# Two-layer attention trunk on one core: later use of turned rows, and the gate's key sums added from DRAM instead of by a matmul

## The chip, the core and the metric

The kernel runs on one core of one Trainium2 chip. The metric is the device time of one execution in microseconds (us), lower is better. The core has five engines with queues of their own, each in order: TensorE (PE; PEld is its weight load), VectorE (DVE), ScalarE (ACT), GpSimd (POOL) and SyncE (SP, which only issues transfers). ScalarE and GpSimd issue transfers too.

## The reference

256 tokens of width 2048 pass two layers. Layer 0 mixes by forgetting attention (FoX, 16 heads of 128), layer 1 by dilated attention (8 heads, three dilation groups, values of width 256). Each mixer is followed by a squared-ReLU MLP of width 8192. All is float32. What matters here, cut from the reference:

```python
# FoX: c is the running sum over tokens of log sigmoid of a gate, one per head
log_f = jax.nn.log_sigmoid((f + b_f).astype(jnp.float32))
c = jnp.cumsum(log_f, axis=1)
c_keys = jnp.transpose(c, (0, 2, 1))
...
s = jnp.einsum('bqhd,bkhd->bhqk', q_i, k) * scale      # q, k RMS-normed per head
s = s + jnp.transpose(c_i, (0, 2, 1))[..., None] - c_keys[:, :, None, :]
s = jnp.where(causal, s, -jnp.inf)
p = jax.nn.softmax(s, axis=-1)
o = jnp.einsum('bhqk,bkhd->bqhd', p, v)
```

So each score gets the query's sum c_i, less the key's sum c_keys, and the causal mask.

## The kernel before

**Products.** Tokens lie in two tiles of 128 (`NT`). Weights come in as raw blocks of 256 rows by 512 columns (`load`, L288, SyncE's queue). `split` makes two parts of each: `wh` by a cast on ScalarE (L309) and the rest `wl` on VectorE (L310), five buffers of each. `product_steps` (L340 to L342) multiplies, for each of 16 values of k and both token tiles, high by high, high by low and low by high: six matmuls of 128x512 a step. After each second step a new block is split, and after each step the clock of the jobs ticks.

**Jobs.** All other work is written as generators. `yield 3` lets three steps pass, and `yield ("fk", j)` waits until that name is done. When a job runs decides where its instructions stand in the engines' queues. `behind(x)` puts a job's instructions behind the instruction x on x's engine; `issued["cast"]`, `issued["cut"]` and `issued["product"]` are the latest cast (L309), cut (L310) and product (L342).

**Queries and keys (`qk_chain`).** After the product of 512 columns, squares on ScalarE give each head's norm; three steps later VectorE normalises (L532) and transposes 32x32 blocks (L540), SyncE writes the blocks to DRAM (L544), and GpSimd's queue reads them back turned (L545, `qn`). After 10 steps, and then 2 and 2, the turned rows of the first and of the second token tile are scaled and copied (L554, L561) on ScalarE, and the rest is taken on VectorE (L563). Then ("fq", j), ("fk", j) or ("dqk", q4, g) is done. The work tiles of a chain are four of the five buffers of the tag "w".

**FoX heads.** Four groups j of four heads: product of queries, of keys, of values, 16 steps each. `gate_chain` makes the running sums `c_q` (by token) once, and from them `negc`, in which rows 0 to 15 and 32 to 47 hold the high and low parts of the 16 heads' negative sums over the keys. `make_sel(j)` builds on GpSimd a selector with ones in the two rows of each head. `fox_head` waits for queries, keys, gate and mask and a number of steps, then L746 multiplies selector and `negc` into a score bank (128x384), on which the scores are accumulated: 128 columns for the first token tile (L657), 256 for the second in three parts (L660). L754 adds `c_q` and the mask on VectorE. Softmax follows; the probabilities are turned by way of DRAM on ScalarE's queue (`p_turned`, L610 and L614), or for the last two heads by TensorE, split (`p_split`, L623 and L625), and multiplied with the values (`pv`, L593, L594). The score banks are two (`ps_sc`), shared with `pv`.

**Dilated heads.** `dil_head` does the same for three groups of scores (L806 adds a table of distances); four rounds q4 of two heads, with three chains of queries and keys in each round. The output projections use the heads in order, the last ones at k = 12 to 15.

Of the kernel before, what the change touches and what calls it, by code (L numbers as in the profile page):

```python
# [89 lines left out]
def trunk(ctx: ExitStack, tc, x, fox_w_in, fox_b_f, fox_q_gain, fox_k_gain, fox_w_out, dil_w_in,  # L90
# [422 lines left out]
    def qk_chain(acc, tag, key, parts):  # L513

        yield (tag, "rstd")
        sq = []
        for t in range(NT):
            s = work.tile([P, NC], F32, tag="w", name=f"sq_{key}_{t}", bufs=5)
            nc.scalar.activation(halves(s), by_column(acc[t]), AF.Square, scale=rstd[tag][:, t:t + 1])
            sq.append(s)  # L520
        ss = small.tile([P, NT, 4], F32, tag="ss", name=f"ss_{key}")
        for t in range(NT):
            nc.vector.tensor_reduce(ss[:, t, :], sq[t].rearrange("p (h d) -> p h d", h=4), AX.X, ALU.add)
        nc.vector.tensor_scalar(ss, ss, 1.0 / P, EPS, ALU.mult, ALU.add)
        rq = small.tile([P, NT, 4], F32, tag="rq", name=f"rq_{key}")
        nc.gpsimd.tensor_tensor(rq, ss, mhalf.rearrange("p (t h) -> p t h", t=NT), ALU.pow)
        yield 3
        qn = []
        for t in range(NT):
            nc.vector.tensor_scalar_mul(rq[:, t, :], rq[:, t, :], rstd[tag][:, t:t + 1])  # L530
            q = work.tile([P, 4, P], F32, tag="w", name=f"qn_{key}_{t}", bufs=5)
            nc.vector.tensor_mul(q.rearrange("p (h g) d -> p h g d", h=2),  # L532
                                 acc[t].rearrange("p (g d h) -> p h g d", h=2, g=2),
                                 rq[:, t, :].rearrange("p (h g) -> p h g", h=2).unsqueeze(3).to_broadcast([P, 2, 2, P]))
            qn.append(q)


        for t in range(NT):
            turned = sq[t].rearrange("p (j h r) -> p j h r", j=4, h=4)
            nc.vector.transpose(turned.rearrange("p j h r -> p h j r"),  # L540
                                qn[t].rearrange("p h (j c) -> p h j c", c=32))
            blocks = dram.tile([4, 32, 4, P], F32, tag="blocks", name=f"blocks_{key}_{t}", bufs=4)
            for i in range(4):
                nc.sync.dma_start(blocks[:, :, i, :].rearrange("j c x -> c j x"), sq[t][32 * i:32 * i + 32].rearrange("p (j x) -> p j x", j=4))  # L544
            nc.gpsimd.dma_start(qn[t], blocks.rearrange("j c i x -> (j c) (i x)").rearrange("p (h d) -> p h d", h=4))  # L545
        yield 10
        for t in range(NT):
            yield 2
            for n, (c, nh, gcol, (whole, hi, lo)) in enumerate(parts):
                keys = hi.shape[2] == S  # L550
                src = qn[t].rearrange("p i (h r) -> p h i r", h=4)[:, c // P:c // P + nh]
                to = sq[0].rearrange("p (n i x) -> p n i x", n=2, i=2)[:, n] if t else whole
                with behind(issued["cast"]):
                    nc.scalar.activation(to.rearrange("p h (i r) -> p h i r", i=4), src, AF.Copy, scale=gain[:, gcol:gcol + 1])  # L554
                if t == 0 and not keys:
                    continue
                at = slice(t * P, (t + 1) * P) if keys else slice(0, P)

                a, b = (x[:, :, at].rearrange("p i (h n) -> p i h n", h=2) for x in (hi, lo))
                of = to.rearrange("p i (n h) -> p i h n" if keys else "p i (h n) -> p i h n", h=2)  # L560
                nc.scalar.copy(a, of)  # L561
                with behind(issued["cut"]):
                    nc.vector.tensor_sub(b, of, a.bitcast(F32))  # L563
        jobs.done.add(key)
# [85 lines left out]
        v_hi, v_lo = (work.tile([P, NC], F32R, tag=f"v{x}", name=f"{name}{x}", bufs=1) for x in "hl")  # L650
        return whole, v_hi, v_lo

    def scores(ps, t, q, k, i, onto=False):

        (q_whole, q_hi, q_lo), (k_whole, k_hi, k_lo) = q, k
        if t == 0:
            nc.tensor.matmul(ps[:, 0:P], q_whole[:, i, :], k_whole[:, i, :], start=not onto, stop=not onto)  # L657
            return
        for x, (a, b) in enumerate(((q_hi, k_hi), (q_hi, k_lo), (q_lo, k_hi))):
            nc.tensor.matmul(ps[:, P:3 * P], a[:, i, :], in_turn(b[:, i, :], P // 2), start=not onto and x == 0, stop=x == 2)  # L660


    c_q = const.tile([P, NT, FH], F32, name="c_q")

    negc = const.tile([P, 3 * P], F32R, name="negc")

    def gate(tag):
        pf = ps_sc.tile([2 * FH, S], F32, tag="sc", name="pf")
# [5 lines left out]
    def gate_chain(tag, pf):  # L674
# [46 lines left out]
        pct = ps_sc.tile([FH, S], F32, tag="sc", name="pct")  # L721
        for t in range(NT):
            nc.tensor.transpose(pct[:, t * P:(t + 1) * P], c_q[:, t, :], ident)
        ct = work.tile([FH, S], F32, tag="s", name="g_ct", bufs=S_BUFS)
        nc.vector.tensor_scalar(ct, pct, -1.0, None, ALU.mult)
        zero = work.tile([P, 3 * P], F32, tag="s", name="g_zero", bufs=S_BUFS)
        nc.vector.memset(zero, 0.0)
        nc.vector.tensor_copy(negc, zero)
        keys = by_column(ct, P // 2)
        high, low = (negc[at:at + FH, :] for at in (0, 32))  # L730
        nc.vector.tensor_copy(halves(high[:, P:], P // 2), keys)
        nc.vector.tensor_sub(halves(low[:, P:], P // 2), keys, halves(high[:, P:], P // 2).bitcast(F32))
        for part in (high, low):
            nc.vector.tensor_copy(part[:, 0:P], part[:, P:2 * P].bitcast(F32))
        jobs.done.add("gate")

    def fox_head(j, hh, qT, kT, vt, sel):
        h = 4 * j + hh
        yield ("fq", j)
        yield ("fk", j)  # L740
        yield "gate"
        yield "mask"
        yield ((0, 2, 4, 7) if j == 3 else (0, 4, 8, 12))[hh] + 2
        ps = ps_sc.tile([P, 512], F32, tag="sc", name=f"sc_f{h}")
        with behind(issued["product"]):
            nc.tensor.matmul(ps[:, 0:3 * P], sel[:, hh, :], in_turn(negc, P // 2), start=True, stop=False)  # L746
        for t in range(NT):
            scores(ps, t, qT[hh // 2], kT[hh // 2], hh % 2, True)
        s = work.tile([P, 3 * P], F32, tag="s", name=f"s_f{h}", bufs=S_BUFS)
        nm = small.tile([P, NT], F32, tag="nm", name=f"nm_f{h}")  # L750
        den = small.tile([P, NT], F32, tag="den", name=f"den_f{h}")
        spans = [slice(0, P), slice(P, 3 * P)]
        for t in range(NT):
            nc.vector.scalar_tensor_tensor(s[:, spans[t]], ps[:, spans[t]], c_q[:, t, h:h + 1],  # L754
                                           tables["mask"][:, spans[t]], ALU.add, ALU.add)
        for t in range(NT):
            nc.vector.tensor_reduce(nm[:, t:t + 1], s[:, spans[t]], AX.X, ALU.max, negate=True)
        yield 1
# [11 lines left out]
        else:  # L770
            turned = yield from p_turned(s, f"f{h}")
            yield ("fv", j)
            pt_sb = p_split(turned, f"f{h}")
        yield 2
        if ("f", h // 2) not in oT:
            oT["f", h // 2] = tuple(
                act.tile([P, 2, S], F32R, tag=f"aT{x}", name=f"oTf{x}_{h}", bufs=KC // 2) for x in "hl")
# [1 line left out]
        yield from pv(pt_sb, vt, [hh * P], [hi[:, h % 2, :]], [lo[:, h % 2, :]], f"f{h}")  # L779
        jobs.done.add(("of", h))  # L780

    def make_sel(j):
        sf = work.tile([P, 4, P], F32, tag="w", name=f"self{j}", bufs=5)
        nc.gpsimd.memset(sf, 0.0)
        for base in (0, 32):
            nc.gpsimd.affine_select(out=sf, in_=sf, compare_op=ALU.not_equal, fill=1.0, base=-base - 4 * j,
                                    pattern=[[-1, 4], [0, P]], channel_multiplier=1)
        sel = work.tile([P, 4, P], F32R, tag="sel", name=f"sel{j}", bufs=1)
        nc.vector.tensor_copy(sel, sf)
        return sel  # L790


    def dil_head(q4, i, qTs, kTs, vt):
        h = 2 * q4 + i
        for g in range(3):
            yield ("dqk", q4, g)
        yield (3 if q4 == 3 else 6) * i + 2
        s = work.tile([P, 3, 3 * P], F32, tag="sd", name=f"sd{h}", bufs=1)
        for g in range(3):
            yield ("table", g)  # L800
# [26 lines left out]
        else:  # L827
            turned = yield from p_turned(p, f"d{h}")
            yield ("dv", q4)
            pt_sb = p_split(turned, f"d{h}")  # L830
        yield 2
        hi, lo = (act.tile([P, 2, S], F32R, tag=f"aT{x}", name=f"oTd{x}_{h}", bufs=KC // 2) for x in "hl")
        oT["d", h] = hi, lo
        yield from pv(pt_sb, vt, [i * S, i * S + P], [hi[:, 0, :], hi[:, 1, :]], [lo[:, 0, :], lo[:, 1, :]], f"d{h}")
# [148 lines left out]

    tag = "n0"
    for j in range(4):
        sel = make_sel(j)
        qT = [heads_pair(f"fqT{j}_{i}", i, False) for i in range(2)]
        kT = [heads_pair(f"fkT{j}_{i}", 3 + i, True) for i in range(2)]
        vt = values(f"fv{j}")
        product(keys_h(tag), lhs_h(tag), lambda acc: qk_chain(  # L990
            acc, tag, ("fq", j), [(0, 2, FOX_G, qT[0]), (2 * P, 2, FOX_G, qT[1])]))
        if j == 0:
            jobs.need("wf")
            gate(tag)
        product(keys_h(tag), lhs_h(tag), lambda acc: qk_chain(
            acc, tag, ("fk", j), [(0, 2, FOX_G + 1, kT[0]), (2 * P, 2, FOX_G + 1, kT[1])]))

        for hh in range(4):
            jobs.spawn(fox_head(j, hh, qT, kT, vt, sel))
        product(keys_h(tag), lhs_h(tag), lambda acc: v_chain(acc, tag, ("fv", j), vt))  # L1000

    out_proj(lambda k: ("of", k),
# [40 lines left out]
```

## Time and profile before

| what | value |
|---|---|
| median of 3 runs | 2165.43 us (2164.36 to 2166.1) |
| profiled execution | 2163.54 us, its span 2161.8 us |
| TensorE busy | 2145.2 us (99%), 11145 matmuls |
| VectorE busy | 1407.9 us (65%) |
| ScalarE busy | 1098.2 us (51%) |
| GpSimd busy | 75.7 us (4%) |
| transfers | 467.62 MB, mean 216 GB/s |
| mean granted TensorE clock | 0.998 |

A matmul's duration overlaps the next one's, so what one costs is the distance between two starts. PE's idle time is what is left of the span; the view of waits says who ended it. FoX scores run from 85 us of the span, the last FoX head ends at 325 us; the dilated queries and keys begin with the squares at 1090 us, and the last dilated head ends at 1436 us.

### The profile page before, as it was taken

Reading aid. Unit: us, or ns where it says so; the run is one execution under the profiler, and the core shown is the slowest. Engines: PE = TensorE matmul, PEld = TensorE weight load, DVE = VectorE, ACT = ScalarE, POOL = GpSimd, SP = SyncE. Lnnn points to the kernel's source line nnn. Section 1 sums busy time; section 2 is a strip of 40 time slices with the busy share of each in tenths; the row PEclk is TensorE's granted clock in tenths of the full one; section 3 lists DMA queues with packets and bytes.
Section 4 is the critical chain, followed back from the end, with each engine's and each line's share of the span. In section 5 each row is a group of like instructions: output and inputs, shape, how many; then the busy total and the mean of one; then the engine's idle time right before and its main releaser. Section 6 shows DMA issues by size and latency. Waiting matters only on the chain.

```text
span 2161.8 us, 30098 instructions
## 1 busy us (share of the span) xinstructions
PE 2145.2 (99%) x11145; PEld 1908.7 (88%) x11145; DVE 1407.9 (65%) x1883; ACT 1098.2 (51%) x1524; POOL 75.7 (4%) x92
## 2 busy tenths in 40 slices
PE   9999999999999999999999999999999999999999
PEld 7888888998998998998888888888988988988988
DVE  6877778765665565566667878677655655655664
ACT  6555555644444454454555555646544544543542
POOL 1111000000000000000011010100000000000000
PEclk9999999999999999999999999999999999999999
DMA  7777767866666666667777777758666666666664
GB/s 251 237 237 207 256 209 226 263 202 202 202 203 201 202 203 205 199 201 238 248 235 224 251 235 212 259 181 286 204 203 201 201 204 202 199 204 204 200 212 144
DMA packets 307475, 467.62 MB, mean 216 GB/s; under 512 B 34376, under 2 KB 119552, under 8 KB 307328
## 3 DMA queue, kind: packets, MB, share of 16 engines
q1 hardware_dynamic: 288416, 446.27, 65.6%
q10 hardware_dynamic: 15680, 8.92, 1.5%
q0 software_dynamic: 3232, 10.50, 1.4%
q8 instruction: 87, 1.43, 0.3%
q14 instruction: 60, 0.49, 0.1%
HBM read 442.61 MB, written 23.00 MB: 215 GB/s over the span
## 4 chain that ended last, share of the span: by engine, by line
PE 92%; DVE 3%; DMA 2%; ACT 1%; issue 1%; POOL 0%; SPq 0%; DVEq 0%; ACTq 0%; POOLq 0%
PE acc L341 19%; PE acc L340 19%; PE acc L342 19%; PE up_n1a_acc L404 5%; PE up_n3a_acc L404 5%; PE up_n1a_sc L404 3%; PE up_n1a_tp L404 3%; PE up_n3a_tp L404 3%; PE up_n3a_sc L404 3%; PE up_n3a_acc L408 3%; PE up_n1a_acc L408 3%; PE up_n3a_sc L408 1%; PE up_n3a_tp L408 1%; PE up_n1a_tp L408 1%; PE up_n1a_sc L408 1%; DVE wl L310 1%
## 5 line engine op out<-in xcount | busy, mean ns | idle before, releaser
L310 DVE TENSOR_TENSOR wl<-raw,wh 128x1024 fp32r<-128x1024 f32 (+1 forms) x801 | 974.9, 1222 | 654.0 <-ACT wh L309 652.4
L309 ACT CAST wh<-raw 128x1024 fp32r<-128x1024 f32 (+1 forms) x801 | 837.4, 1048 | 939.3 <-PE acc L342 552.0
L340 PE MATMUL acc<-wh,hT_n 128*128 128x512 f32 x896 | 342.4, 383 | 0.3 <-ACT wh L309 0.3
L341 PE MATMUL acc<-wl,hT_n 128*128 128x512 f32 x896 | 341.2, 381 | 0.1
L342 PE MATMUL acc<-wh,hT_n 128*128 128x512 f32 x896 | 340.4, 380 | 0.0
L340 PE MATMUL acc<-wh,aTh_n1a 128*128 128x512 f32 x512 | 194.0, 379 | 0.0
L341 PE MATMUL acc<-wl,aTh_n1a 128*128 128x512 f32 x512 | 194.0, 379 | 0.0
L342 PE MATMUL acc<-wh,aTl_n1a 128*128 128x512 f32 x512 | 194.0, 379 | 0.0
L340 PEld LDWEIGHTS acc<-wh,hT_n 128*128 128x128 f32 x896 | 170.0, 190 | 23.7 <-ACT wh L309 0.7
L342 PEld LDWEIGHTS acc<-wh,hT_n 128*128 128x128 f32 x896 | 170.0, 190 | 23.7
L341 PEld LDWEIGHTS acc<-wl,hT_n 128*128 128x128 f32 x896 | 170.2, 190 | 22.9 <-DVE wl L310 0.4
L340 PE MATMUL acc<-wh,aTh_n3a 128*128 128x512 f32 x480 | 181.9, 379 | 0.0
L341 PE MATMUL acc<-wl,aTh_n3a 128*128 128x512 f32 x480 | 181.9, 379 | 0.0
L342 PE MATMUL acc<-wh,aTl_n3a 128*128 128x512 f32 x480 | 181.9, 379 | 0.0
L404 PE MATMUL up_n1a_acc<-hT_n,wh 128*128 128x512 f32 x512 | 181.6, 382 | 0.0
L404 PE MATMUL up_n3a_acc<-hT_n,wh 128*128 128x512 f32 x512 | 181.6, 382 | 0.0
L408 PE MATMUL up_n1a_acc<-hT_n,wl 128*128 128x256 f32 x512 | 139.6, 273 | 0.0
L408 PE MATMUL up_n3a_acc<-hT_n,wl 128*128 128x256 f32 x512 | 139.6, 273 | 0.0
L341 PEld LDWEIGHTS acc<-wl,aTh_n1a 128*128 128x128 f32 x512 | 96.8, 189 | 13.8
L342 PEld LDWEIGHTS acc<-wh,aTl_n1a 128*128 128x128 f32 x512 | 96.8, 189 | 13.7
L340 PEld LDWEIGHTS acc<-wh,aTh_n1a 128*128 128x128 f32 x512 | 96.8, 189 | 13.6
L404 PEld LDWEIGHTS up_n3a_acc<-hT_n,wh 128*128 128x128 f32 x512 | 96.8, 189 | 13.5
(735 smaller groups left out, 3195.3 us busy)
## 6 DMA issues: line engine op xcount, KB each, us to landing
raw<-in_mlp_w_up_dram SPq DMA_DIRECT2D x256, 512.0 KB, 4.3
raw<-in_mlp_w_down_dram SPq DMA_DIRECT2D x256, 512.0 KB, 4.0
raw<-in_dil_w_in_dram SPq DMA_DIRECT2D x192, 256.0 KB, 4.1
raw<-in_fox_w_in_dram SPq DMA_DIRECT2D x95, 512.0 KB, 4.8
raw<-in_fox_w_out_dram SPq DMA_DIRECT2D x32, 512.0 KB, 4.9
raw<-in_dil_w_in_dram SPq DMA_DIRECT2D x32, 512.0 KB, 5.7
raw<-in_dil_w_out_dram SPq DMA_DIRECT2D x32, 512.0 KB, 5.0
blocks_n<-turned_n SPq DMA_DIRECT2D x96, 64.0 KB, 2.1
```

Of the source, the lines that this page charges most:

```text
L309: issued["cast"] = nc.scalar.copy(hi[:, part, :], raw[:, part, :])
L310: issued["cut"] = nc.vector.tensor_sub(lo[:, part, :], raw[:, part, :], hi[:, part, :].bitcast(F32))
L340: nc.tensor.matmul(acc[t], ah[:, tok], hi, start=first, stop=False)
L341: nc.tensor.matmul(acc[t], ah[:, tok], lo, start=False, stop=False)
L342: issued["product"] = nc.tensor.matmul(acc[t], al[:, tok], hi, start=False, stop=last)
L404: issued["product"] = nc.tensor.matmul(banks[b], hi[:, i, col], in_turn(tokens.rearrange("p x s -> p (x s)"), P // 2), start=first, stop=last)
L408: nc.tensor.matmul(banks[b][:, 0:S], lo[:, i, col], in_turn(tokens[:, 0, :], P // 2), start=False, stop=False)
```

## The change

- `qk_chain`: 12 steps instead of 10 between the transposition's transfers and the use of the turned rows.
- `fox_head` and `dil_head`: 3 steps instead of 2 between the split of the probabilities and `pv`; `dil_head` starts its scores 1 step after its last input instead of 2.
- `negc` is a DRAM tile of 16 rows of 384, written once by SyncE's queue from the negated sums. Each FoX head reads its row into all 128 partitions of `bias` (two buffers) on ScalarE's queue, 4 steps before its scores; the first head of a group does so as soon as the queries are there. VectorE adds the mask into it, and L754's successor adds `bias` in place of the mask.
- The selector, its matmul L746 and the parts of `negc` are gone; all score matmuls of a head stand behind the latest product.

```diff
@@ qk_chain
-        yield 10
+        yield 12
@@ scores: no "onto", the first matmul of each part starts the bank
-    def scores(ps, t, q, k, i, onto=False):
+    def scores(ps, t, q, k, i):
...
-    negc = const.tile([P, 3 * P], F32R, name="negc")
+    negc = dram.tile([FH, 3 * P], F32, tag="negc", name="negc", bufs=1)
@@ gate_chain
-        ct = work.tile([FH, S], F32, tag="s", name="g_ct", bufs=S_BUFS)
-        nc.vector.tensor_scalar(ct, pct, -1.0, None, ALU.mult)
-        zero = work.tile([P, 3 * P], F32, tag="s", name="g_zero", bufs=S_BUFS)
-        nc.vector.memset(zero, 0.0)
-        nc.vector.tensor_copy(negc, zero)
-        keys = by_column(ct, P // 2)
-        high, low = (negc[at:at + FH, :] for at in (0, 32))
-        nc.vector.tensor_copy(halves(high[:, P:], P // 2), keys)
-        nc.vector.tensor_sub(halves(low[:, P:], P // 2), keys, halves(high[:, P:], P // 2).bitcast(F32))
-        for part in (high, low):
-            nc.vector.tensor_copy(part[:, 0:P], part[:, P:2 * P].bitcast(F32))
+        ct = work.tile([FH, 3 * P], F32, tag="s", name="g_ct", bufs=S_BUFS)
+        nc.vector.tensor_scalar(ct[:, P:], pct, -1.0, None, ALU.mult)
+        nc.vector.tensor_copy(ct[:, 0:P], ct[:, P:2 * P])
+        nc.sync.dma_start(negc, ct)
@@ fox_head
-    def fox_head(j, hh, qT, kT, vt, sel):
+    def fox_head(j, hh, qT, kT, vt):
         h = 4 * j + hh
+        at = ((0, 2, 4, 7) if j == 3 else (0, 4, 8, 12))[hh] + 2
         yield ("fq", j)
-        yield ("fk", j)
         yield "gate"
         yield "mask"
-        yield ((0, 2, 4, 7) if j == 3 else (0, 4, 8, 12))[hh] + 2
+        if hh:
+            yield ("fk", j)
+            yield at - 4
+        bias = work.tile([P, 3 * P], F32, tag="bias", name=f"bias{h}", bufs=2)
+        with behind(issued["cast"]):
+            nc.scalar.dma_start(bias, negc[h:h + 1, :].to_broadcast([P, 3 * P]))
+        yield 4
+        nc.vector.tensor_add(bias, bias, tables["mask"])
+        if hh == 0:
+            yield ("fk", j)
+            yield 2
         ps = ps_sc.tile([P, 512], F32, tag="sc", name=f"sc_f{h}")
         with behind(issued["product"]):
-            nc.tensor.matmul(ps[:, 0:3 * P], sel[:, hh, :], in_turn(negc, P // 2), start=True, stop=False)
-        for t in range(NT):
-            scores(ps, t, qT[hh // 2], kT[hh // 2], hh % 2, True)
+            for t in range(NT):
+                scores(ps, t, qT[hh // 2], kT[hh // 2], hh % 2)
...
-                                           tables["mask"][:, spans[t]], ALU.add, ALU.add)
+                                           bias[:, spans[t]], ALU.add, ALU.add)
...
-        yield 2          # between p_split and pv
+        yield 3
@@ make_sel and its calls are gone
@@ dil_head
-        yield (3 if q4 == 3 else 6) * i + 2
+        yield (3 if q4 == 3 else 6) * i + 1
...
-        yield 2          # between p_split and pv
+        yield 3
```

More of the change, by code (lines that the diff above doesn't have):

```diff
@@ L651, in values @@
         return whole, v_hi, v_lo
-    def scores(ps, t, q, k, i, onto=False):
+    def scores(ps, t, q, k, i):
         (q_whole, q_hi, q_lo), (k_whole, k_hi, k_lo) = q, k
         if t == 0:
-            nc.tensor.matmul(ps[:, 0:P], q_whole[:, i, :], k_whole[:, i, :], start=not onto, stop=not onto)
+            nc.tensor.matmul(ps[:, 0:P], q_whole[:, i, :], k_whole[:, i, :], start=True, stop=True)
             return
         for x, (a, b) in enumerate(((q_hi, k_hi), (q_hi, k_lo), (q_lo, k_hi))):
-            nc.tensor.matmul(ps[:, P:3 * P], a[:, i, :], in_turn(b[:, i, :], P // 2), start=not onto and x == 0, stop=x == 2)
+            nc.tensor.matmul(ps[:, P:3 * P], a[:, i, :], in_turn(b[:, i, :], P // 2), start=x == 0, stop=x == 2)
     c_q = const.tile([P, NT, FH], F32, name="c_q")
-    negc = const.tile([P, 3 * P], F32R, name="negc")
+    negc = dram.tile([FH, 3 * P], F32, tag="negc", name="negc", bufs=1)
     def gate(tag):
@@ L780, in fox_head @@
         jobs.done.add(("of", h))
[L782 to L790, printed above, removed]
     def dil_head(q4, i, qTs, kTs, vt):
@@ L985, in trunk @@
     for j in range(4):
-        sel = make_sel(j)
         qT = [heads_pair(f"fqT{j}_{i}", i, False) for i in range(2)]
@@ L998, in trunk @@
         for hh in range(4):
-            jobs.spawn(fox_head(j, hh, qT, kT, vt, sel))
+            jobs.spawn(fox_head(j, hh, qT, kT, vt))
         product(keys_h(tag), lhs_h(tag), lambda acc: v_chain(acc, tag, ("fv", j), vt))
```

## The prediction

> **What bounds the kernel now.** I read the page's first lines, then the waits of TensorE, the timelines of the places they name, and the windows around those.
>
> ```profile
> PE 2145.2 (99%) x11145; PEld 1908.7 (88%) x11145; DVE 1407.9 (65%) x1883; ACT 1098.2 (51%) x1524; POOL 75.7 (4%) x92
> ```
> ```profile
> engine line waited for: us in total, times, longest us
> PE sc_f L660 <- ACT fkT_0h L561: 5.6, 4, 2.5
> PE spare L119 <- POOL ident masks.py:199: 2.5, 1, 2.5
> PE ps_g_mix L138 <- DMA g_mix<-in_mix_norm_g_dram: 2.0, 1, 2.0
> PE po_d L593 <- DVE pTl_d L625: 1.4, 2, 0.7
> PE sc_d L657 <- DVE sd L806: 1.1, 2, 0.8
> PE acc L340 <- ACT wh L309: 0.3, 1, 0.3
> ```
>
> TensorE is busy for 2145.2 us of the span of 2161.8 us, and no weight but the first ever makes it wait. So only two things can move the end: fewer or faster TensorE instructions, and the few waits above. The largest is the change's subject: four times, once per group of four FoX heads, the first score block waits for ScalarE to write the second half of the turned keys, 5.6 us in all. The 1.4 and 1.1 us are the same kind of wait in the dilated layer; the other three belong to the start.
>
> The wait of the second group on TensorE, and what follows it (start, duration, engine; the idle time stands in brackets):
>
> ```profile
> 153.44 0.33 PE L746 MATMUL sc_f<-negc,sel 128*128 128x384 f32 x1
> 153.61 0.38 PE L657 MATMUL sc_f<-fkT_0w,fqT_0w 128*128 128x128 f32 x2
> 155.83 0.38 PE L660 MATMUL sc_f<-fkT_0h,fqT_0h 128*128 128x256 f32 x1 [1.84 <-ACT fkT_0h L561]
> 157.47 0.63 PE L342 MATMUL acc<-wh,hT_n 128*128 128x512 f32 x1
> 157.90 0.63 PE L340 MATMUL acc<-wh,hT_n 128*128 128x512 f32 x1
> 160.98 0.38 PE L342 MATMUL acc<-wh,hT_n 128*128 128x512 f32 x1
> 161.20 0.38 PE L340 MATMUL acc<-wh,hT_n 128*128 128x512 f32 x1
> 226.03 0.38 PE L660 MATMUL sc_f<-fkT_0h,fqT_0h 128*128 128x256 f32 x1 [0.97 <-ACT fkT_0h L561]
> 296.07 0.38 PE L660 MATMUL sc_f<-fkT_0h,fqT_0h 128*128 128x256 f32 x1 [2.50 <-ACT fkT_0h L561]
> ```
>
> Starts count, since durations overlap: 157.47 to 157.90 is 0.43 us a product, 160.98 to 161.20 is 0.22. For a while after the wait TensorE ran at half rate. The windows give the granted clock in the column PEclk:
>
> ```profile
> core 0: us, PE busy (x) PEld busy (x) DVE busy (x) ACT busy (x) POOL busy (x), PEclk, DMA share, GB/s
> 155.90:157.10 1.20, 1.20 (x7) 1.11 (x8) 0.94 (x3) 1.15 (x2) 0.00 (x0) 1.00 0.97 244
> 157.10:160.50 3.40, 3.40 (x10) 2.62 (x10) 3.40 (x7) 1.94 (x5) 0.00 (x0) 0.52 0.54 158
> 226.30:229.70 3.40, 3.40 (x18) 3.01 (x18) 3.14 (x8) 2.49 (x6) 0.00 (x0) 1.00 0.55 189
> 297.20:300.50 3.30, 3.30 (x9) 2.60 (x8) 3.10 (x6) 1.93 (x6) 0.00 (x0) 0.50 0.52 176
> ```
>
> After the waits of 1.84 and 2.50 us the clock was 0.52 and 0.50 for 3.4 and 3.3 us; after the wait of 0.97 us it stayed at 1.00. Half of those 6.7 us, about 3.3 us, was lost on top of the waits, so the four waits cost 5.6 + 3.3 = 8.9 us. The Trainium skill, "TensorE: Matmul & The Clock Gate", section "Why this matters for your kernels", asks for no idle gaps over about 3 us. By that rule gaps of 1.84 and 2.50 us would leave the clock alone; the trace disagrees, and I go by the trace.
>
> **Why ScalarE is late.** The last group, first SyncE's queue, then ScalarE:
>
> ```profile
> 278.70 1.77 SPq L544 DMA_DIRECT2D blocks_('fk', 3)_0_2877<-sq_('fk', 3)_0_2828  x4
> 282.54 16.48 SPq L288 DMA_DIRECT2D raw<-in_fox_w_out_dram  x9
> ```
> ```profile
> 281.57 1.05 ACT L309 CAST wh<-raw 128x1024 fp32r<-128x1024 f32 x1 [1.54 <-PE acc L342]
> 288.85 1.05 ACT L309 CAST wh<-raw 128x1024 fp32r<-128x1024 f32 x1 [6.23 <-DMA raw<-in_fox_w_out_dram]
> 290.13 1.05 ACT L309 CAST wh<-raw 128x1024 fp32r<-128x1024 f32 x1 [0.23 <-DMA raw<-in_fox_w_out_dram]
> 292.71 1.04 ACT L309 CAST wh<-raw 128x1024 fp32r<-128x1024 f32 x1
> 295.61 0.41 ACT L561 CAST fkT_0h<-sq_('fk', 3)_0_2828 128x256 fp32r<-128x256 f32 x1
> ```
>
> SyncE's queue is in order. The keys' blocks wait there for VectorE's transpose until 278.70, the weight loads stand behind them until 282.54, and the next cast waits 6.23 us for its weights. The casts have a lead of up to five buffers over TensorE, so products don't notice, but the turned keys are queued on ScalarE behind those casts and arrive at 295.61.
>
> **The change, part by part.** A step below is one k of a product on two token tiles: six 128x512 products at 0.22 us (161.20 less 160.98), 1.3 us; two steps are 2.6 us, with one cast of weights.
>
> *The selector.* Sixteen products of 384 columns go. From the start of L746 to that of L657 is 0.17 us (153.44 to 153.61), so 16 x 0.17 = 2.7 us of pure TensorE time. Nothing hides it and nothing replaces it on TensorE: **-2.7 us**.
>
> *10 to 12 steps, FoX.* The second-half step (L554, L561, L563) and the scores behind it both move two steps later, so the distance between them stays. What changes is how far ScalarE has caught up. TensorE gets there 2.6 us later; ScalarE has one more cast in front, 1.05 us, if its weights are there by then (the loads leave SyncE nine in 16.48 us, 1.8 us each, faster than the 2.6 us in which they are used). A wait thus shrinks by 1.54 us: 2.50 to 0.96, 1.84 to 0.30, 0.97 and the first group's to nothing. Left are 1.3 us, and none is longer than the 0.97 us that kept the clock at 1.00, so the half-rate stretches go too: 8.9 less 1.3 is **-7.6 us**. Bounds: -8.9 if every wait goes; nothing, or below, if VectorE's work or the loads slip along (rivals).
>
> What else moves: the t=1 step of a queries' chain now falls on the step at which the next chain normalises and transposes (16 + 3 = 3 + 12 + 2 + 2 steps), and both draw on the five "w" buffers; VectorE's L563 stand ahead of that transpose. On the other side the t=0 step no longer stands on ScalarE ahead of the next chain's squares (one step before them till now, one after). I take these as even.
>
> *The dilated layer.* Chain +2, head -1: scores one step later, p.v two (another +1 from 2 to 3). The two waits on pTl_d, 1.4 us, get a step more each, 1.3 us against 0.7: gone. The sd waits (1.1 us) are for one of two score banks that VectorE frees late, behind a transposition; a step later it may be free or not:
>
> ```profile
> 1160.66 0.55 DVE L806 SCALAR_TENSOR_TENSOR sd<-dist,sc_d 128x384 f32<-128x384 f32 x1
> 1161.73 0.70 DVE L540 STREAM_TRANSPOSE sq_('dqk', 1, 0)_0_10618<-qn_('dqk', 1, 0)_0_10669 128x512 f32<-128x512 f32 x1
> 1162.35 0.67 DVE L540 STREAM_TRANSPOSE sq_('dqk', 1, 0)_1_10620<-qn_('dqk', 1, 0)_1_10672 128x512 f32<-128x512 f32 x1
> ```
>
> The nearest score bank is freed here at 1161.2; behind both transposes it would be 1163.6, 2.4 us later, less 1.3 for the step: 1.1 us worse. I put the layer at **-1.1 us**, between -2.5 (both kinds go) and -0.3 (the pTl_d waits go, the sd waits grow by 1.1).
>
> *The rows from DRAM.* Sixteen bias transfers of 192 KB on ScalarE's queue, and 16 additions of 128x384 on VectorE. The nearest rows are the same size, from DRAM on the same queue, and an addition of the same shape:
>
> ```profile
> turned_f<-pblocks_f ACTq DMA_DIRECT2D x14, 192.0 KB, 3.3
> ```
> ```profile
> L821 DVE TENSOR_TENSOR p_d<-p_d,sd x8: 557/557/558, 1168.3 to 1422.8; 128x384 f32<-128x384 f32 x8
> ```
> ```profile
> DVE sel L789 <- PE sc_f L746: 5.3, 3, 1.8
> DVE sel L789 <- POOL self L786: 4.4, 1, 4.4
> ```
>
> 3.3 us to landing against four steps, 5.2 us, between transfer and addition: covered, by 1.9 us, as long as ScalarE issues on time. 16 x 0.56 = 8.9 us are added to VectorE, which is 65% busy; against it stand 9.7 us in which it waited for the selector's copies. What stands behind an addition that waits is a cut (L310) or s_f (L754); the cuts' lead covers the first. On ScalarE the third head of the last group finds its bias buffer in use until the first head's L754, and its own exponentials come behind that anyway. On SyncE one store of negc waits for the gate one step before the first keys' blocks, which wait there longer. On POOL the masks of the selector go from ahead of the keys' return. Sum here: **0 us**, between +1.0 (a head late) and -1.0.
>
> *The end of both layers.* The output projections first use the last heads' p.v at k=12 and 13, 40 and 41 steps after the last chain's product. They now come at 35 and 37 (FoX), and 37 and 38 (dilated): three steps to spare at the least, 3.9 us. No cost.
>
> **Sum.** -2.7 - 7.6 - 1.1 = -11.4 us. The profiled execution took 2163.54 us (its span 2161.8 and 1.7 around it), 1.9 us under the median of 2165.43. 2163.5 - 11.4 = 2152.1, and by the median **2154.0 us**.
>
> **Rivals.**
> - *The lateness moves along.* If VectorE's transposes fall two steps later with the merged step, SyncE's loads start later by as much, and the four waits stay. Then only the selector counts, 2165.4 - 2.7 = 2162.7 us. For it: the queue order above, and the coincidence of the two chains. Against: the transposition's own start (step 3) is not moved by the diff. Chance 0.20.
> - *Slower: the banks.* In the dilated layer and the FoX groups the score bank waits on VectorE behind the merged step. If that puts each second block behind both transposes and the L563, each of eight groups waits 2.5 us (like the longest now) and cools, 1.7 us more: 8 x 4.2 = 33.6 us against 8.9 + 2.5 that stand there now and 2.7 gained, 20 us slower, 2185; it decides once three of the eight do so while the FoX waits stay. For it: the 0.8 us wait at 1160. Against: of the eight dilated heads two wait so now, 1.1 us together. Chance 0.10.
> - *The clock is not the waits'.* If the half-rate stretches came for a reason other than these waits, 3.3 us are not regained: 2157.3 us. Against: the two follow the two longest waits, and none follows the shorter ones. It is what the Trainium skill's section named above would lead to. Chance 0.05.
> - *My forecast*, 0.65; by itself 2151 (every wait gone: -2.7 - 8.9 - 2.5 = -14.1) to 2159.
>
> **Numbers.** 0.2% is 4.3 us, about what a measurement of this kernel tells from no change. Faster holds the forecast, the clock rival and a small part of the first rival (some waits shorter): 0.73. Same: the rest of it, 0.17. Slower: 0.10. The range, 2150 to 2164, takes in the first rival and leaves out the banks.
>
> **What would show it.** L746 gone; the wait of sc_f on fkT_0h under 1.5 us in all; granted clock near 1.00 right after each first head; additions of bias with no idle time of VectorE over 1 us before them; SyncE's fk blocks no later than now against the group's scores. I am wrong if sc_f still waits 2 us anywhere, if sc_d waits more than 3 us in all, or if ScalarE's casts wait for bias transfers.

## The result, and the profile after

| kernel | median, us | runs, us | ratio to before, 95% interval |
|---|---|---|---|
| before | 2165.66 | 2162.54 to 2169.52 | |
| changed | 2161.2 | 2155.88 to 2165.61 | 0.9977 [0.9969, 0.9985] |

The change gains 4.5 us, 0.23%, under half of the 11.4 us forecast. Each median is that of 15 executions; of all kernels below only e2 had executions far outside the rest, two of twelve at 5742.19 and 12825.42 us, which are left out of its median and ratio. The profiled execution took 2161.2 us, its span 2159.5 us, 2.3 us less than the span before.

The page's line of the engines, the changed kernel:

```profile
PE 2142.0 (99%) x11129; PEld 1905.7 (88%) x11129; DVE 1411.1 (65%) x1890; ACT 1098.5 (51%) x1524; POOL 66.0 (3%) x80
```

The sixteen selector products are gone (11145 to 11129). TensorE's waits:

```profile
engine line waited for: us in total, times, longest us
PE po_f L593 <- ACT pTh_f L623: 4.8, 2, 3.4
PE sc_d L657 <- DVE sd L799: 3.1, 3, 2.7
...
PE sc_f L660 <- ACT fkT_0h L561: 1.0, 1, 1.0
```

The wait on the turned keys, the change's subject, fell from 5.6 to 1.0 us, and the pTl_d wait is no longer in the view. In their place stands a wait that the kernel before did not have: FoX p.v waits for the cast of the turned probabilities, 4.8 us, and the dilated score bank costs 3.1 us instead of 1.1. The second group's keys and its last head's p.v on TensorE:

```profile
156.43 0.39 PE L657 MATMUL sc_f<-fkT_0w,fqT_0w 128*128 128x128 f32 x2
156.57 0.36 PE L660 MATMUL sc_f<-fkT_0h,fqT_0h 128*128 128x256 f32 x1
...
195.90 0.38 PE L342 MATMUL acc<-wh,hT_n 128*128 128x512 f32 x1
199.65 0.58 PE L593 MATMUL po_f<-pTh_f,fv1h 128*128 128x256 f32 x1 [3.37 <-ACT pTh_f L623]
200.02 0.64 PE L340 MATMUL acc<-wh,hT_n 128*128 128x512 f32 x1
200.45 0.63 PE L341 MATMUL acc<-wl,hT_n 128*128 128x512 f32 x1
```

Where 1.84 us were waited before, the two score parts now follow each other by 0.14 us. But 40 us later TensorE waits 3.37 us, and then its starts are 0.43 us apart (200.02 to 200.45) instead of 0.22. The windows (PEclk is the granted clock):

```profile
core 0: us, PE busy (x) PEld busy (x) DVE busy (x) ACT busy (x) POOL busy (x), PEclk, DMA share, GB/s
199.70:206.00 6.30, 6.30 (x19) 5.29 (x20) 4.51 (x6) 5.16 (x9) 0.00 (x0) 0.54 0.67 201
297.30:300.60 3.30, 2.59 (x12) 2.19 (x13) 2.80 (x6) 2.22 (x5) 0.00 (x0) 1.00 0.73 234
```

The half-rate stretches after the second and the fourth group's keys are gone (1.00 at 297.3), and a new one follows the new wait: 0.54 over these 6.3 us, 2.9 us lost.

So the two profiled spans differ by the selector's 2.7, 4.6 of key waits, 3.3 of their half-rate stretches and 1.4 of pTl_d, against 4.8 of p.v waits, 2.9 of a new half-rate stretch and 2.0 more of score banks: -12.0 + 9.7 = -2.3 us, as measured.

**Why p.v waits.** TensorE, ScalarE and its queue (ACTq) at that place, changed kernel:

```profile
190.85 0.39 PE L594 MATMUL po_f<-turned_f,fv1w 128*128 128x128 f32 x2
191.27 0.37 ACT L596 CAST oTfh<-po_f 128x256 fp32r<-128x256 f32 x1 [2.96 <-PE po_f L594]
191.49 0.34 ACTq L614 DMA_DIRECT2D turned_f<-pblocks_f  x1
199.19 0.41 ACT L623 CAST pTh_f<-turned_f 128x256 fp32r<-128x256 f32 x1 [3.58 <-DMA turned_f<-pblocks_f]
```

L596 copies out the second head's output and waits for TensorE to finish it; the return of the last head's probabilities (L614) stands behind it on ScalarE's queue. It leaves at 191.49 and takes 7.6 us, between weight loads. In the DMA view of 185 to 205 us that return, first before, then changed (times, KB, us to landing):

```profile
turned_f<-pblocks_f ACTq DMA_DIRECT2D x1, 192.0 KB, 2.6
```
```profile
turned_f<-pblocks_f ACTq DMA_DIRECT2D x1, 192.0 KB, 7.6
```

Counted in the kernels' instruction order, the second group's heads stand at these steps on TensorE (scores of the last head; p.v of the second head from its first to its last part; p.v of the last head):

```
                              scores   p.v, 2nd head    p.v, last head
before                         111      120.3 - 121.7    128.7 - 129.0
rows alone (e1)                111      122.2 - 123.0    128.8 - 129.3
changed                        113      123.2 - 125.2    128.5 - 129.5
rows and chain of 12 (e7)      113      123.2 - 125.2    129.5 - 130.0
changed, last p.v late (e3)    113      123.2 - 125.2    132.0
changed, GpSimd returns (e12)  113      122.5 - 125.2    129.0 - 129.5
```

The last head's scores move two steps later and its p.v does not: 15.5 steps between them instead of 17.7. The second head's p.v, behind which the return is held, ends 3.5 steps later. No run shows why the order puts these heads there.

### The profile page after: what moved, and what is told of

The parts are those of the page before. It is cut to its first block, busy times and chain, and to the rows that moved or that the text cites. A ratio compares the mean times of both kernels' runs of the same rounds, so it can differ in the third digit from the quotient of the medians.

```text
span 2159.5 us, 30045 instructions
## 1 busy us (share of the span) xinstructions
PE 2142.0 (99%) x11129; PEld 1905.7 (88%) x11129; DVE 1411.1 (65%) x1890; ACT 1098.5 (51%) x1524; POOL 66.0 (3%) x80
## 4 chain that ended last, share of the span: by engine, by line
PE 91%; DMA 3%; DVE 2%; ACT 1%; issue 1%; SPq 0%; POOL 0%; ACTq 0%; DVEq 0%; POOLq 0%
PE acc L340 19%; PE acc L341 19%; PE acc L342 19%; PE up_n3a_acc L404 5%; PE up_n1a_acc L404 5%; PE up_n3a_sc L404 3%; PE up_n3a_tp L404 3%; PE up_n1a_tp L404 3%; PE up_n1a_sc L404 3%; PE up_n1a_acc L408 3%; PE up_n3a_acc L408 3%; PE up_n1a_sc L408 1%; PE up_n1a_tp L408 1%; PE up_n3a_tp L408 1%; PE up_n3a_sc L408 1%; DMA raw<-in_dil_w_in_dram 1%
## 5 line engine op out<-in xcount | busy, mean ns | idle before, releaser
L310 DVE TENSOR_TENSOR wl<-raw,wh 128x1024 fp32r<-128x1024 f32 (+1 forms) x801 | 974.4, 1220 | 645.2 <-ACT wh L309 643.3
L404 PEld LDWEIGHTS up_n1a_acc<-hT_n,wh 128*128 128x128 f32 x512 | 96.8, 189 | 13.5
```

Source lines behind the costliest of these rows:

```text
L310: issued["cut"] = nc.vector.tensor_sub(lo[:, part, :], raw[:, part, :], hi[:, part, :].bitcast(F32))
L404: issued["product"] = nc.tensor.matmul(banks[b], hi[:, i, col], in_turn(tokens.rearrange("p x s -> p (x s)"), P // 2), start=first, stop=last)
```

## The experiments

Each ratio is to the kernel before, measured beside it (medians 2166.24, 2164.59 and 2165.32 us for e1 to e4, e5 to e8 and e9 to e12); the gain is the difference of the medians. The ratio is not the quotient of the medians, and where the executions scatter the two differ: for e3 it is 8.2 us by the ratio and 9.8 by the medians.

| run | median, us | ratio, 95% interval | gain, us |
|---|---|---|---|
| e1 rows alone | 2155.85 | 0.9951 [0.9938, 0.9965] | 10.4 |
| e2 steps alone | 2163.02 | 0.999 [0.9981, 1.0] | 3.2 |
| e3 changed, last p.v late | 2156.43 | 0.9962 [0.995, 0.9973] | 9.8 |
| e4 changed, first dilated scores late | 2157.13 | 0.996 [0.9948, 0.9972] | 9.1 |
| e5 rows alone, dead masks | 2153.84 | 0.9949 [0.9936, 0.9962] | 10.8 |
| e6 before, masks off "w" | 2164.3 | 0.9995 [0.9986, 1.0005] | 0.3 |
| e7 rows and chain of 12 | 2161.04 | 0.9982 [0.9972, 0.9993] | 3.6 |
| e8 rows, dilated scores later | 2159.73 | 0.9976 [0.9966, 0.9985] | 4.9 |
| e9 rows alone, cut first | 2159.28 | 0.9976 [0.9966, 0.9986] | 6.0 |
| e10 before, no selector product | 2160.2 | 0.9977 [0.9968, 0.9985] | 5.1 |
| e11 rows alone, dilated p.v 3 | 2152.43 | 0.9944 [0.9931, 0.9958] | 12.9 |
| e12 changed, return on GpSimd | 2153.59 | 0.9949 [0.9937, 0.9962] | 11.7 |

### The two halves: e1 and e2

e1 is the changed kernel with the old step counts, e2 the kernel before with the new ones.

```diff
-        yield 12          # e1: qk_chain
+        yield 10
-        yield 3           # e1: ahead of pv, both layers
+        yield 2
-        yield (3 if q4 == 3 else 6) * i + 1    # e1: dil_head
+        yield (3 if q4 == 3 else 6) * i + 2
```

> The sums come from DRAM, all step counts as before. The selector's 16 matmuls go (16 x 0.16 us = 2.6 us); the four key waits, their half-rate stretches and the small dilated waits stay. My theory: 2163 us beside 2165.5, i.e. -2 to -4 us, sc_f on fkT_0h still 4 to 6 us in all, no wait of po_f on pTh_f over 0.5 us, sc_d on sd about 1 us. Rival (the transfers of the bias rows themselves make the turned probabilities late): po_f waits on pTh_f here too, 3 us or more, and the gain is below 1 us.

> Only the step counts change, the selector stays. My theory (the new po_f and sd waits come with the steps, not with the rows): sc_f on fkT_0h about 1 us, po_f on pTh_f 2 to 6 us, sc_d on sd about 3 us; time about as before, 2164 to 2166 us. Rival (the rows' transfers make the new waits): po_f and sd waits as before, time 2157 us.

TensorE's waits of e1, then of e2:

```profile
PE sc_d L657 <- DVE sd L799: 4.0, 3, 3.4
...
PE po_d L593 <- DVE pTl_d L625: 1.4, 2, 0.7
PE sc_f L660 <- ACT fkT_0h L561: 0.6, 1, 0.6
```
```profile
PE sc_d L657 <- DVE sd L806: 4.5, 2, 4.3
PE po_f L593 <- ACT pTh_f L623: 3.2, 3, 1.8
```

Without any extra step the rows end the key waits (5.6 to 0.6 us) and gain 10.4 us, where I had priced them at the selector's 2.7. The steps alone end them as well, but bring the p.v waits and gain 3.2, with an interval that reaches 1.0. Each half removes the same waits; together they remove them once, and the price of the steps is paid on top: 4.5 us instead of 10.4.

### What the rows did to the keys: e5, e6, e9, e10

e5 keeps `make_sel` as dead work in e1 (and puts `bias` into the tags "t1" and "t2"); e6 takes the masks out of the "w" buffers of the kernel before.

```diff
+        make_sel(j)                                                          # e5, result unused
-        sf = work.tile([P, 4, P], F32, tag="w", name=f"self{j}", bufs=5)     # e6
+        sf = work.tile([P, 4, P], F32, tag="t1", name=f"self{j}")
```

> The rows from DRAM with the step counts of before, and with the selector's masks still built once per group (GpSimd's fills into a w buffer and VectorE's copy), though no product reads them; the bias row takes a buffer of the tags t1 and t2 to make room. This separates what the selector cost on TensorE and in its scheduled place from what its masks cost on GpSimd, VectorE and the w buffers. Theory A: the key waits went because product steps, a cut and a transpose changed places in VectorE's and TensorE's orders (here those orders around the keys are as in the kernel with the rows alone): sc_f waits under 1.5 us in all, no half-rate stretch, 2155 to 2157 us. Theory B: the masks' own work (a w buffer held, GpSimd ahead of the keys' return, VectorE's copy) made the keys late: sc_f waits 4 us or more again, clock near 0.5 after at least one, 2160 to 2163 us.

> The kernel before, with one edit: the selector's mask tile takes a buffer of the tag t1 in place of one of the five w buffers, which the chains share. Nothing is left out; the sixteen selector products stay. Theory A (order of instructions, not the buffers): the four key waits stay near 5.6 us with both half-rate stretches, 2164 to 2167 us, same as before. Theory B (the mask tile held a w buffer that the chains needed): the waits fall under 2 us and the half-rate stretches go, 2158 to 2160 us.

Theory A by the times of both: building the masks costs nothing (10.8 us gained with them), and giving "w" a buffer gains 0.3 us within its interval. One number of e5 misses: sc_f waited 1.8 us once, though at full clock after it. One of e6 does too: the key waits are 5.1 us, but its profiled execution, the fastest of its eleven, has no half-rate stretch behind them.

e9 is e1 with VectorE's order around the keys as it was before; e10 is the kernel before without L746.

```diff
-            nc.vector.transpose(turned.rearrange("p j h r -> p h j r"),      # e9, in qk_chain
+            with behind(*([issued["cut"]] if key[0] == "fk" else [])):
+                nc.vector.transpose(turned.rearrange("p j h r -> p h j r"),
...
-            nc.tensor.matmul(ps[:, 0:3 * P], sel[:, hh, :], in_turn(negc, P // 2), start=True, stop=False)   # e10
```

> The kernel with the rows alone and the old step counts, with one edit: each keys' transposition (L540, FoX) is put behind the weights' cut that was issued last, so VectorE does cut, transpose, transpose as in the kernel before, where the rows alone have transpose, cut, transpose. TensorE's order stays that of the rows alone, with two or three products between the first score block and the second. Theory A (VectorE's order is the larger part of what the rows brought): the keys' blocks come about 1.2 us later and the waits of sc_f on the turned keys return to 3 to 4 us in all with one half-rate stretch, 2158 to 2161 us. Theory B (the products that TensorE has between the two score blocks are the larger part): sc_f under 2 us in all, no half-rate stretch, 2155 to 2157 us as with the rows alone.

> The kernel before without its sixteen selector products (L746): the gate's sums of the keys are left out of the scores, all else of the selector (masks, copy, rows on the chip) stays. VectorE's order around the keys is that of before; TensorE now has two or three products between the score blocks of the second and third group, none in the last group. Theory A (the waits need VectorE's order to change too): the last group still waits 2 us or more with a half-rate stretch, the second about 1.3 us: sc_f 3 to 4.5 us in all, 2159 to 2162 us. Theory B (taking the product from TensorE is all that the rows brought): sc_f under 1.5 us, no half-rate stretch, 2154 to 2156 us. My prediction's step by itself (the products' own 2.7 us, waits unchanged): 2162 us.

VectorE at the last group's keys, first before, then e1, then SyncE's loads behind them in e1:

```profile
276.23 0.69 DVE L532 TENSOR_TENSOR qn_('fk', 3)_1_2874<-acc,rq_('fk', 3)_2836 128x512 f32<-128x512 f32 x1
276.83 1.22 DVE L310 TENSOR_TENSOR wl<-raw,wh 128x1024 fp32r<-128x1024 f32 x1
277.97 0.71 DVE L540 STREAM_TRANSPOSE sq_('fk', 3)_0_2828<-qn_('fk', 3)_0_2871 128x512 f32<-128x512 f32 x1
```
```profile
268.65 0.69 DVE L532 TENSOR_TENSOR qn_('fk', 3)_1_2855<-acc,rq_('fk', 3)_2815 128x512 f32<-128x512 f32 x1
269.26 0.70 DVE L540 STREAM_TRANSPOSE sq_('fk', 3)_0_2807<-qn_('fk', 3)_0_2852 128x512 f32<-128x512 f32 x1
269.88 1.18 DVE L310 TENSOR_TENSOR wl<-raw,wh 128x1024 fp32r<-128x1024 f32 x1
```
```profile
273.79 2.14 SPq L288 DMA_DIRECT2D raw<-in_fox_w_out_dram  x4
```

In e1 the first transpose stands ahead of the cut L310. It isn't the loss of the selector's copy that does this: e5 keeps the copy on VectorE and has the order of e1. What in the rows does it stays open. From L532 until SyncE is free for the loads it took 282.54 - 276.23 = 6.3 us before and 273.79 - 268.65 = 5.1 us in e1, since SyncE now issues the first blocks while VectorE cuts. It is the queue order that the prediction showed as the cause of ScalarE's lateness, shorter by about one cut. The same stretch, from the start of the later L532 to the first load behind the blocks, and the wait of the first score block on fkT_0h, both read from the timelines for groups two, three and four:

```
                            L532 to loads, us    wait on the keys, us
before                      6.3   6.3   6.3      1.84   0.97   2.50
masks off "w" (e6)          6.3   6.3   6.3      2.39   0.97   1.73
no selector product (e10)   6.3   6.3   5.2      2.38   0.49   0.66
rows, cut first (e9)        6.9   7.4   7.1      1.15   1.25   2.67
rows alone (e1)             5.1   5.1   5.1      0.10   0      0.64
rows, dead masks (e5)       5.1   5.3   5.2      0.10   0      1.81
steps alone (e2)            5.2   5.2   5.2      0      0      0
changed                     5.2   5.2   5.2      0      0      1.03
```

Putting the cut first again costs 10.4 - 6.0 = 4.4 us, and the key waits of e9 are back. Its loads leave later than those of the kernel before, so 4.4 us is likely more than the old order alone would cost:

```profile
PE sc_f L661 <- ACT fkT_0h L562: 5.1, 3, 2.7
```

So theory A's time came and more than its waits, but not its half-rate stretch: after the longest wait, 2.7 us, products were 0.22 us apart. In e10 the key waits are 4.7 us and the gain 5.1 us, more than the products' own 2.7. The waits lie elsewhere than expected: 1.1 us in the first group, 2.4 in the second, with a half-rate stretch, and 0.7 in the last. VectorE's order was meant to stay, and did in the second and third group; in the last the cut moved ahead of the later L532, the loads left 1.1 us earlier, and the wait of 2.50 us shrank to 0.66. That speaks for theory A once more. Part of the gain may be order on TensorE, where two or three products (0.4 to 0.7 us) now stand between the first and the second score block of groups two and three; no run tells it apart from the scatter of the runs.

### Which step costs: e7, e3, e12

e7 is e1 with the 12 in `qk_chain` alone. e3 and e12 each edit one thing in the changed kernel.

```diff
-        yield 3                                            # e3, fox_head
+        yield 8 if j < 3 and hh == 3 else 3
...
-        with behind(issued["cast"]):                       # e12, FoX only
-            nc.scalar.dma_start(turned.rearrange("p i b r -> p (i b r)"), blocks.rearrange("j c i x -> (j c) (i x)"))
+        nc.gpsimd.dma_start(turned.rearrange("p i b r -> p (i b r)"), blocks.rearrange("j c i x -> (j c) (i x)"))
```

> The rows from DRAM, and of the step changes only the 12 for 10 in the chain that turns queries and keys; the p.v stays at 2 steps after its weights and the dilated scores at their old offset. Theory A (the later chain pushes the last head's scores toward a p.v that does not move as far, and ScalarE's queue holds its return behind the second head's output): po_f waits on pTh_f 2 us or more with a half-rate stretch after the longest, 2158 to 2162 us, near the changed kernel. Theory B (the 3 for 2 in front of p.v and the dilated offsets are what cost): no po_f wait over 1 us, 2154 to 2157 us, like the rows alone at 2155.9.

> The changed kernel, with the last head of the first three FoX groups multiplying its probabilities 5 steps later (8 steps instead of 3 after its split). My theory (the return transfer of that head is issued late on ScalarE's queue, lands late among the weight loads, and only this head's place on TensorE is too early for it): the po_f waits of 4.8 us and the half-rate stretch behind them (2.7 us) go, 6 to 7.5 us off the profiled execution of the changed kernel, median about 2155.5. Rival (ScalarE and the loads as a whole are late there, so the next step in line waits instead): another wait of 2 us or more appears in the same place and the gain is under 2 us.

> The changed kernel with one edit: the FoX heads' return of the turned probabilities (L614) is issued from GpSimd's queue in place of ScalarE's. TensorE's order around p.v stays within half a step. Theory A (the return stood on ScalarE behind the copy of the second head's output, which waits for TensorE): it is issued as soon as its blocks have landed, the po_f waits on pTh_f fall from 4.8 us to under 1 us, the half-rate stretch goes, 2155 to 2158 us. Theory B (the transfer is slow because it meets the weight loads, whoever issues it): po_f waits stay at 3 us or more, 2160 to 2162 us.

e7's waits:

```profile
PE po_f L593 <- ACT pTh_f L623: 2.4, 1, 2.4
...
PE po_d L593 <- ACT pTh_d L623: 1.8, 1, 1.8
```

The 12 alone takes 6.8 of the rows' 10.4 us away and brings the p.v wait, here in the first group and with no half-rate stretch behind it; the 3 for 2 is not needed for it. In the second group its last p.v stands a step later than in the changed kernel and doesn't wait. The two profiled spans, 2157.6 and 2155.0 us, are 2.6 us apart, so the profiles show less than half of the 6.8. e3, with the last p.v 2.5 to 3.5 steps later, ends the p.v waits and gains 9.8. Its profiled execution took 2163.3 us, 6.9 over its median, with sd waits of 5.1 and sc_f waits of 3.2 us, so those are no measure of the median. e12 decides between queue and landing. Its last head:

```profile
186.66 0.54 POOL L614 DMA_DIRECT2D turned_f<-pblocks_f  x1
...
189.16 0.37 ACT L596 CAST oTfh<-po_f 128x256 fp32r<-128x256 f32 x1 [8.46 <-PE po_f L594]
...
194.49 0.35 PE L593 MATMUL po_f<-pTh_f,fv1h 128*128 128x256 f32 x1
```

The return leaves 2.5 us before L596 instead of 0.2 us behind it. It still takes long to land (6.3 us here, 7.6 in the changed kernel), but no p.v wait is among TensorE's rows any more, and only the score bank's is left of any length:

```profile
PE sc_d L660 <- DVE sd L802: 2.5, 2, 2.3
...
PE sc_f L663 <- ACT fkT_0h L561: 0.2, 1, 0.2
```

With that one edit the changed kernel gains 11.7 us, against 4.5 without it. Theory A holds; the slow landing is a part of the wait, but was not enough to cause it once the issue came earlier. The kernel is faster than the 2155 to 2158 us expected. The last p.v stands half a step later than in the changed kernel, 0.65 us, too little to end a wait of 3.37 us by itself.

### The dilated layer: e4, e8, e11

```diff
-        yield (3 if q4 == 3 else 6) * i + 1                              # e4, in the changed kernel
+        yield (3 if q4 == 3 else 6) * i + (4 if q4 == 0 else 1)
-        yield (3 if q4 == 3 else 6) * i + 2                              # e8, in e1
+        yield (3 if q4 == 3 else 6) * i + (9 if q4 == 0 else 2)
-        yield 2                                                          # e8 and e11: ahead of dilated pv
+        yield 3
```

> The changed kernel, with the scores of the first round's dilated heads 3 steps later (4 instead of 1). My theory (the score bank is freed by VectorE only behind the next chain's normalising and transposing): the 2.7 us wait at 1160 us goes, sc_d on sd falls from 3.1 to about 0.5 us in all, 2.5 us off, median about 2158.5. Rival (the bank is late whatever the place, since the first scores' own inputs are late): the wait moves along and nothing is gained.

> An attempt at a better version: the rows from DRAM with the old step counts in the FoX layer; in the dilated layer p.v 3 steps after its weights, and the first group's scores 9 steps after its chain in place of 2, so that they come after VectorE's work on the next chain and after the landing of the raw weights. Theory A (the 4.0 us of sd waits and 1.4 us of pTl_d waits that the rows alone left are a matter of distance): sd under 1.5 us, pTl_d under 0.5 us in all, 2151 to 2154 us. Theory B (VectorE frees the score banks late wherever the scores stand): sd stays at 2 to 4 us, 2154 to 2157 us, no better than 2155.9.

> The rows alone with the old step counts, and of the step changes only the 3 for 2 ahead of the dilated layer's p.v: an attempt at a version better than both. In TensorE's order it moves only the start of the second head's p.v by one step, the scores stay where they are. Expected if the wait on pTl_d is a matter of that step: pTl_d from 1.4 us to under 0.3 us, all else as with the rows alone, 2153.5 to 2155.5 us. If the lateness moves along as it did with the scores moved too: pTl_d 1.4 us or more, 2156 us or slower.

e4 did not end the wait that it was made for (sd 2.9 us in its profile) and is inconclusive as to its gain: its runs lie from 2155.0 to 2164.0, and its profile still has 6.0 us of p.v waits, which its edit doesn't touch. e8 came out slower than either theory had it. It shows a rescheduled wait: sd falls to 0.9 us, and the p.v behind it waits instead, with a half-rate stretch.

```profile
PE po_d L593 <- ACT pTh_d L623: 3.3, 1, 3.3
PE po_d L593 <- DVE pTl_d L625: 2.6, 3, 1.2
```

e11 has the lowest median of the study, 2152.43 us, with runs from 2151.67 to 2152.95 and an interval that overlaps those of e1, e5 and e12, but not for the reason expected:

```profile
PE po_d L593 <- DVE pTl_d L625: 1.4, 2, 0.7
PE sc_d L657 <- DVE sd L799: 1.0, 2, 0.7
```

The pTl_d wait is as long as before. What differs from e1 is the bank's wait, 1.0 instead of 4.0 us, and in e1 that wait was followed by a half-rate stretch. The scores stand at the same places in both orders, so I cannot say that the edit caused it. e5, with the old count, has the same waits (pTl_d 1.5, sd 0.9 us) and 2153.84.

## Why the prediction was right or wrong

- *Selector, -2.7.* Right in kind; the sixteen products went and nothing replaced them on TensorE. e10 gives 5.1 us, with the changes of order that come with it.
- *10 to 12 steps, -7.6.* As a term for the wait it named, the number holds: 2.50 was to become 0.96 and measured 1.03; 1.84 and 0.97 went; the clock after the key scores is 1.00. That it came so near is partly luck. The loads also left SyncE 1.1 us earlier, in the changed kernel and with the steps alone, where the prediction took VectorE's moves as even, and no kernel here has twelve steps without that; the 1.54 us a wait is shown by none. The step that failed is the one that counted this as the whole effect: "what else moves" and the end of the layers took p.v to follow the yields, with three steps to spare. In TensorE's order the last head's p.v stayed at 128.5 while its scores moved from 111 to 113, and its return waits on ScalarE behind the second head's output. That cost 4.8 us and 2.9 of clock in the profile. I had looked at the queues that the turned keys pass, and not at ScalarE's queue for the probabilities. The steps' sum was to be -8.7 with the dilated layer's; alone it measured -3.2 (e2), and on top of the rows +5.9 (10.4 less 4.5).
- *The rows from DRAM, 0.* The second step that failed. With the selector's 2.7 the rows alone were to gain 2.7 us; they gained 10.4. The cost side was about right: VectorE waited 11.2 us in 7 of the sixteen additions, up to 3.3 us, so the forecast of no idle time over 1 us was wrong, but none of it shows among TensorE's waits. What I had at nothing was that VectorE would take the transpose ahead of a cut, so that SyncE's loads leave 1.2 us earlier and the key waits fall to 0.6 us: likely no more than 4.4 us (e9 against e1). With it went the half-rate stretches of 3.3 us, which e9's profile does not bring back.

```profile
DVE bias L744 <- DMA bias<-negc: 11.2, 7, 3.3
```

- *The dilated layer, -1.1.* The pTl_d waits went as forecast; the sd waits grew by 2.0 us, over the 1.1 of the bound, to 3.1 us in all, over the 3 us that the prediction named as a sign of being wrong. While TensorE waits from 1159.9 us on, the bank's release stands behind both transposes and a cut, so the place of the bank rival is real, 2.7 us, in one group of eight and not in three.

```profile
1160.24 0.67 DVE L540 STREAM_TRANSPOSE sq_('dqk', 1, 0)_1_10603<-qn_('dqk', 1, 0)_1_10652 128x512 f32<-128x512 f32 x1
1160.83 1.18 DVE L310 TENSOR_TENSOR wl<-raw,wh 128x1024 fp32r<-128x1024 f32 x1
1161.94 1.01 DVE L799 SCALAR_TENSOR_TENSOR sd<-dist,sc_d 128x384 f32<-128x384 f32 x2
```

- *The rivals.* The median, 2161.2, lies nearest to "the lateness moves along" (2162.7), but not by its mechanism: the key waits did go. That the median lies inside the range is luck, since the range reaches so far up for waits on the keys, and no rival named a wait of p.v. "The clock is not the waits'" is not borne out: in the changed kernel the stretches went with their waits, and a new one came with the new wait. But the price was not certain: in e6 and e9 waits of 2.39 and 2.67 us had no stretch behind them.
- *The sum, -11.4.* e12 gained 11.7 with all of the change in it and the return moved to another queue. So about the sum is there once p.v doesn't wait, but its nearness is partly luck: in e12's profile the dilated layer, forecast at -1.1, loses its 1.4 us of pTl_d waits and pays 1.4 more of score banks and 1.7 for a half-rate stretch behind them. That the rows remove the same key waits as the steps does not change it, since a wait goes only once.

## What to carry to other kernels

When a step is moved in an order that the program's waits and an in-order queue share, follow the moved head to its last use, and list for each transfer on the way what stands ahead of it on the queue that issues it: here a 192 KB return stood behind a copy that waited for TensorE. A wait that two edits can each remove is gained once; test the edits alone, since the cheaper one may be enough. An edit can also pay by what changes place on another engine: here 2.7 us of products went, and up to 4.4 us hung on one changed place on VectorE, so read the order of every engine again after it.

## What the runs showed of the hardware

- **The clock after a wait.** Over the fourteen profiles shown or named here, all 6 waits of TensorE over 3 us (3.30 to 4.55) were followed by a half-rate stretch, none of the 12 from 0.97 to 1.73 us, and of the 15 from 1.81 to 2.74 us seven: 1.84, 1.94, 1.98, 2.23, 2.27, 2.38 and 2.50 were, 1.81, 1.82, 1.83, 2.35, 2.37, 2.39, 2.67 and 2.74 were not. The two waits of each profile's first 10 us are left out. In the trace's record of the clock each of these 13 stretches stands at 0.50 and lasts 3.41 us, or 6.83 in three of them; five of the 13 begin before the wait has ended. My prediction took a half-rate stretch as certain from 1.84 us up. The Trainium skill, "TensorE: Matmul & The Clock Gate", section "Why this matters for your kernels", asks for no gaps over about 3 us; the runs agree above 3 us, and show that 1.8 us can already be too long.
- **Spread.** Kernels with waits of that length scatter: the changed kernel over 9.7 us in 15 runs (its mean clock from 1.000 in the run of 2155.88 to 0.997 in that of 2165.61), e11 and e12, with at most one such wait, over 1.3 and 1.9 us in five runs each.
- **Landing.** The same 192 KB return took 2.6, 6.3 and 7.6 us at the same place of three kernels (before, e12, changed), with the DMA engines busy for 0.72, 0.89 and 0.96 of that time. In e12 another queue issues it, and no run takes the load apart from that.
